# Three gates of a two-stream transformer layer: multiplied on ScalarE, added up on GpSimd, in place of VectorE

## The chip, the cores and the metric

The kernel runs on one core of a Trainium2 chip. The metric is the device time of one execution in microseconds; of before it is the median of three runs. The engines are called PE (TensorE), DVE (VectorE), ACT (ScalarE), POOL (GpSimd) and SP (SyncE, which here only issues transfers).

## The reference

One layer for two streams of 128 tokens by 2048 features, a prompt and a sample. Both go through the same weights, each with its own modulation: a conditioning vector times `w_ada` gives six vectors of 2048 features (a shift, a scale and a gate for the mixer, and the same for the feed-forward part).

```python
def adaln_params(cvec, w_ada_l, b_ada_l):
    mod = jax.nn.silu(cvec) @ w_ada_l + b_ada_l
    return jnp.split(mod[..., None, :], 6, axis=-1)
...
def ffn_residual(x, shift, scale, gate, norm_w, wg, wu, wd):
    h = modulate(rmsnorm(x, norm_w), shift, scale)
    return x + gate * ((jax.nn.silu(h @ wg) * (h @ wu)) @ wd)
...
    sh1, sc1, g1, sh2, sc2, g2 = mods
    hq, hi, hff, hfb, hg, cb, cc, cx, nq, nk, nv = mixer_inputs(x, sh1, sc1, norm_mix_w_l, w_in_l)
...
    x = x + g1 * (jnp.concatenate([o_a, o_b, o_c], axis=-1) @ w_out_l)
    x = ffn_residual(x, sh2, sc2, g2, norm_ffn_w_l, wg, wu, wd)
```

The input projection feeds a gated linear recurrence in both directions, a short convolution and an attention; their outputs go through `w_out`. Everything is float32. The change touches only how parts of `g1` and `g2` are summed.

## The kernel before

The weights (330 MB read in all) stream through once, in tiles of 128 partitions by 2048 values (1 MB), and both streams' products are made from each. A float32 product is made of three float32r ones: SP loads a tile into `raw` (four buffers), ACT copies each half of it to `hi` rounded to float32r (L253, L296), DVE subtracts (`lo = raw - hi`, L254, L297), and PE multiplies with both (L262 in `products`, L311 in `feature_mm`). `hi` and `lo` have three buffers each, of half a tile (1024 values a partition).

In time: first norm, the first modulation and input projection to about 555 us, output projection to 640, second norm, then the channel mixer: gate and up weights of six of the eleven hidden tiles (650 to 919 us), down weights (to 1050), gate and up of the other five (to 1274), down (to 1383), last norm.

The modulation has 24 chunks of 512 features. The first eight (first shift and scale) are made ahead of all. The later ones are made beside the stream: behind each tile of weights `behind` calls `pump` (one step of every generator that waits) and `ada_step`, which takes parts from two queues at a pace that a table sets for each phase. `LATER_T` goes to PE (`later_pe`). `LATER_V`, seven chunks that are gates (8 to 11 of the output projection, 21 to 23 of the down projection), goes to DVE in `later_dve`: each chunk in eight parts. A part loads two rows of 128 of `w_ada` (`araw`, 512 KB, two buffers) by a transfer that POOL issues (L415), behind a copy of two elements (L414) that marks the buffer, and then DVE does four sums (L418), for two rows and two streams:

```python
nc.vector.scalar_tensor_tensor(acc[:, s, :], raw[:, k, :], cs[:, 2 * part + k, s:s + 1], acc[:, s, :],
                               op0=ALU.mult, op1=ALU.add)
```

So each partition sums its own rows into `acc` (`aacc`, one buffer). After the eighth part `later_gate` splits the sum as well (ACT L376, DVE L377), PE adds over the partitions with a matrix of ones (L382), and ACT copies the gate out (L383). In all 56 parts and 224 sums.

Instructions on each engine run in the order that a scheduler gave them at build time; it simulates the program and lets weights' steps go ahead of others by a priority. An engine that waits for an instruction's operands holds everything behind it.

`u4` is a ring of tiles of 1024 values for intermediate results, of nine buffers. Two of the chunk-20 quarters are loaded into four of them at the end of the output projection (L924 to L926, on SP's queue).

Of the kernel before, what the change touches and what calls it, by code (L numbers as in the profile page):

```python
# [28 lines left out]
# Chunks of the later modulation that the tensor engine takes (the shift and the scale of the same features in turn),  # L29
# and those that the vector engine takes (gates).  # L30
# [3 lines left out]
RAW_BUFS, HL_BUFS, U8_BUFS, U4_BUFS, ST_BUFS = 4, 3, 10, 9, 4  # L34
# [3 lines left out]
# Tiles of the later modulation per tile of the other weights: in the input projection's last round of the first  # L38
# chunks, its other chunks, the output projection and the channel mixer.
# [4 lines left out]
def pairs(t, m, slot0=0):  # L44
    """View of a [P, 2, n, 128] tile: even blocks of m from the first slot, odd ones from the second."""
    b = t[:, :, :, :]
    n = b.shape[2] * b.shape[3]
    return bass.AP(tensor=b.tensor, offset=b.offset,
                   ap=[list(b.ap[0]), [2 * m, n // (2 * m)], [n + m, 2], [1, m]])
# [9 lines left out]
def half_blocks(t, slot, par, m):  # L59
    """Blocks of m with parity par in one slot of a [P, 2, n, 128] tile: [P, blocks, m]."""  # L60
    b = t[:, :, :, :]
    n = b.shape[2] * b.shape[3]
    return bass.AP(tensor=b.tensor, offset=b.offset + slot * n + par * m,
                   ap=[list(b.ap[0]), [2 * m, n // (2 * m)], [1, m]])


def sibling(t, slot, par, m, nb):
    """Per-block values [P, 2, nb] of one slot and parity, repeated along m: [P, nb / 2, m]."""
    b = t[:, :, :]
    return bass.AP(tensor=b.tensor, offset=b.offset + slot * nb + par,  # L70
                   ap=[list(b.ap[0]), [2, nb // 2], [0, m]])


def sibling_pairs(t, m, nb):
    """Odd values of the first slot, even ones of the second, repeated along m: [P, nb / 2, 2, m]."""
    b = t[:, :, :]
    return bass.AP(tensor=b.tensor, offset=b.offset + 1,
                   ap=[list(b.ap[0]), [2, nb // 2], [nb - 1, 2], [0, m]])


def bc_last(ap, n):
    """[P, a] or [P, a, b] repeated n times along a new last axis."""
    return bass.AP(tensor=ap.tensor, offset=ap.offset, ap=[list(x) for x in ap.ap] + [[0, n]])


def bc_mid(ap, n):
    """[P, a] repeated n times along a new middle axis: [P, n, a]."""
    return bass.AP(tensor=ap.tensor, offset=ap.offset,
                   ap=[list(ap.ap[0]), [0, n]] + [list(x) for x in ap.ap[1:]])
# [3 lines left out]
def trunk(ctx: ExitStack, tc: tile.TileContext, a: dict):  # L93
# [71 lines left out]
    def other_inputs(after):  # L165
        """The small inputs that nothing needs at first; after: a tile that is written first."""
        lvf = st((P, 5, 32))
        selbf = st((P, 2, P))
        for dst, src in ((nfw, a["nfw"]), (gnw, a["gnw"]), (lvf, a["lvl"]), (cvw, a["cvw"]),
                         (selbf, a["selb"])):  # L170
            v = dst if len(dst.shape) == 2 else dst[:, 0, :]
            nc.gpsimd.tensor_copy(v[:, 0:1], after[:, 0:1])
            nc.gpsimd.dma_start(dst, src)
        yield
        yield
        nc.vector.tensor_copy(lvl, lvf)
        nc.vector.tensor_copy(selb, selbf)
        nc.vector.tensor_scalar(ones, ident, 0.0, 1.0, op0=ALU.mult, op1=ALU.add)
        nc.vector.reciprocal(lbs, lbe)
        nc.vector.tensor_tensor(lbe, lbe, lbs, op=ALU.mult)  # L180
        nc.vector.tensor_tensor(lb, lbe, lbe, op=ALU.subtract)
        nc.vector.tensor_scalar(oml, lb, -1.0, 1.0, op0=ALU.mult, op1=ALU.add)

    def rsqrt(v, n):
        """v ** -0.5 of a positive [P, n]: a first guess from the exponent, then Newton's steps."""
        g = sb([P, 8], "rs_g", 2)[:, :n]
        t = sb([P, 8], "rs_t", 2)[:, :n]
        nc.vector.tensor_scalar(g.bitcast(I32), v.bitcast(I32), 1, None, op0=ALU.logical_shift_right)
        nc.vector.tensor_scalar(g.bitcast(I32), g.bitcast(I32), -1.0, float(0x5F3759DF), op0=ALU.mult, op1=ALU.add)
        for _ in range(3):  # L190
            nc.vector.tensor_tensor(t, g, g, op=ALU.mult)
            nc.vector.scalar_tensor_tensor(t, t, -0.5, v, op0=ALU.mult, op1=ALU.mult)
            nc.vector.scalar_tensor_tensor(g, t, 1.5, g, op0=ALU.add, op1=ALU.mult)
        return g

    def rms1(ssq, width, rest=EPS):
        """1 / sqrt(ssq / width + rest) of a [P, 1], times RMS1: Newton's steps without their factors."""
# [14 lines left out]
    def rms(ssq, n, width):  # L212
        """1 / sqrt(ssq / width + eps)."""
        v = sb([P, 8], "rs_v", 2)[:, :n]
        nc.vector.tensor_scalar(v, ssq, 1.0 / width, EPS, op0=ALU.mult, op1=ALU.add)
        return rsqrt(v, n)

    def most(ssq):
        """All sums of squares but the last, as rms1 adds them."""
        t = sb([P, 1], "most", 2)  # L220
        nc.vector.tensor_reduce(t, ssq, axis=AX.X, op=ALU.add)
        nc.vector.tensor_scalar(t, t, 1.0 / D, EPS, op0=ALU.mult, op1=ALU.add)
        return t

# [13 lines left out]
    def split(src, apart=False):  # L238
        """The two float32r parts of a tile of weights, two rows of 128 at a time."""
# [18 lines left out]
    def products(acc, s, k, lhs, lk, parts, first, last):  # L258
        """acc += lhs[s][lk] @ row k of a tile of weights; lhs: [P, s, hi/lo, 4, 128]."""
        hi, lo = parts[k // 2]  # L260
        for i, (x, w) in enumerate(((0, hi), (1, hi), (0, lo))):
            nc.tensor.matmul(acc, lhsT=lhs[:, s, x, lk, :], rhs=w[:, k % 2, :],  # L262
                             start=first and i == 0, stop=last and i == 2)

    def split_mm(src, acc, lhs, first, last, k0=0):
        """acc[s] += lhs[s][k] @ src[:, k]; src: [P, k, 512] of DRAM; lhs: [P, s, hi/lo, 4, 128], from its k0 on."""
# [6 lines left out]
    def last_mm(steps, acc, phase):  # L273
        """The last of a sum, one stream after the other; yields the stream that is done."""
# [10 lines left out]
    def feature_mm(src, rhs, accs2, first, last):  # L285
        """accs2[b] += src[:, k, b].T @ the tokens; src: [P, 8, 256] of DRAM.

        rhs(k): either [P, 512], their two parts, that stay apart, or two of [P, s, 128], that are summed."""
# [30 lines left out]
    def ada_pe(src, box, part, pieces, first, last):  # L319
        """A quarter of a chunk of the modulation on the tensor engine, in four parts g.  # L320

        pieces: (columns, row): the chunk's columns whose sums go to rows 32 g + row + s."""
# [21 lines left out]
    def columns(e, n):  # L344
        """[P, 128 n]: the sums of two modulations in its rows -> [P, n, 2 and 2] by features."""
# [21 lines left out]
    def later_gate(c, parts, pe):  # L367
        """parts[s]: [P, 512] whose sum over partitions (those of s) is the modulation."""
# [19 lines left out]
    def later_pe(c, part, box):  # L388
        """A quarter of a chunk on the tensor engine: a gate, or the second shift and scale, both into one sum."""
# [14 lines left out]
    def later_dve(c, part, box):  # L404
        """An eighth of a gate's chunk on the vector engine, each partition summing its own rows."""
# [10 lines left out]
        for k in range(2):  # L416
            for s in range(2):
# [31 lines left out]
    def behind(phase=None):  # L449
        """What follows a tile of weights."""  # L450
# [4 lines left out]
    def transposes(src):  # L455
        """[128 tokens, 512] in SBUF -> [128, 4, 128] in PSUM."""
# [6 lines left out]
    def split_fm(dst, s, src):  # L463
        """dst: [P, s, hi/lo, 4, 128] tile; src: [P, 4, 128], in PSUM or SBUF."""
# [3 lines left out]
    def norm_fm(xn, diag=None):  # L468
        """xn[s]: [128, 256] in SBUF -> [128, s, 2, 128] in PSUM, its tokens scaled by a diagonal matrix."""
# [9 lines left out]
    def modulated(dst, ps, layer, v):  # L479
        """The modulated norm's features 256 v .. of both streams into dst."""  # L480
# [30 lines left out]
    hT = [None] * 4  # L511

    def first_mod(v, part, box):
        """The first shift and scale of 256 features, a quarter of the sum at a time, and what they modulate."""
# [31 lines left out]
    def heads(t, h):  # L546
        """Head h of a [P, (s, 4 heads), 128] tile: [P, s, 128]."""
# [421 lines left out]
    def hidden(c, f):  # L969
        """256 features of the hidden layer, by features, into a half of f."""  # L970
# [37 lines left out]
    for gi, grp in enumerate(groups):  # L1008
# [6 lines left out]
        for n in range(4):  # L1015
# [8 lines left out]
            for s in last_mm([(a["w_down"][n, grp[j]], fs[j]) for j in range(many, len(grp))], acc, 3):  # L1024
# [105 lines left out]
```

## Time and profile before

| | us |
|---|---|
| median of three runs | 1398.59 (1397.38 to 1398.76) |
| span of the profiled execution | 1393.3 |
| PE busy | 1352.9 |
| DVE busy | 908.2 |
| ACT busy | 652.5 |
| POOL busy | 138.9 |

The profile gives the profiled execution by its span, from the first instruction to the last; no device time of that one execution stands beside it. The span is 5.3 us under the median of the runs. The page's second part cuts the span into 40 slices of 34.8 us: PE shows 9 (90% or more) in 38 of them, and DVE's digits are 8 or 9 in the slices of the input projection, where its other work meets the gates' sums, and 5 to 6 in the last third.

In the rows below, an instruction is named by its line in the code, the engine, the operation, and what it writes `<-` what it reads.

### The profile page before, as it was taken

The page shows a single profiled execution, that of the slowest core. Times are in us where ns is not written, and L with a number is a line of the kernel's source. Part 1 is how long each engine was busy: PE and PEld are TensorE (multiplying, and loading weights), DVE is VectorE, ACT ScalarE, POOL GpSimd, SP SyncE. Part 2 cuts the span into 40 slices and gives each one's busy share as a digit, 9 for nine tenths or more (in the row PEclk, how much of TensorE's full clock was granted, in tenths as well). Part 3 has the DMA queues.
Part 4 walks back from the last instruction along what each step waited for, and adds up shares of the span by engine and source line. Part 5 has one row for each costly group of instructions (what it writes and reads, how often), then busy time and mean ns, then how long its engine had stood idle before and what let it go on. Part 6 is the DMA issues. An engine that isn't in the chain of part 4 may idle for free. (4 is left out here: it accounts for less than half of the span.)

```text
span 1393.3 us, 21206 instructions
## 1 busy us (share of the span) xinstructions
PE 1352.9 (97%) x8552; PEld 1103.2 (79%) x8552; DVE 908.2 (65%) x1190; ACT 652.5 (47%) x927; POOL 138.9 (10%) x201
## 2 busy tenths in 40 slices
PE   5999999999999999999999999999999999999996
PEld 3666767897897896678888887888888888888885
DVE  3354568987967886468958788555555555555565
ACT  4433347655455433446454444543334444444442
POOL 1000002321222230001202121000000000000000
PEclk9999999999999999999999999999999999999999
DMA  8897877775877898765755666555556555555551
GB/s 349 294 359 273 317 304 272 293 268 212 304 274 264 318 348 317 265 263 198 282 198 213 242 215 230 186 185 189 203 183 220 197 186 181 185 194 196 183 203 67
DMA packets 54386, 335.48 MB, mean 241 GB/s; under 512 B 7248, under 2 KB 7312, under 8 KB 19216
## 3 DMA queue, kind: packets, MB, share of 16 engines
q1 hardware_dynamic: 42768, 296.79, 57.9%
q0 software_dynamic: 10944, 36.29, 7.3%
q8 instruction: 67, 1.10, 0.3%
q10 hardware_dynamic: 576, 1.05, 0.2%
q14 instruction: 31, 0.25, 0.0%
HBM read 330.43 MB, written 3.67 MB: 240 GB/s over the span
## 5 line engine op out<-in xcount | busy, mean ns | idle before, releaser
L311 PE MATMUL acc<-u,hi 128*128 128x512 f32 (+1 forms) x2176 | 629.3, 357 | 0.0
L311 PE MATMUL acc<-u,lo 128*128 128x256 f32 x1792 | 488.4, 282 | 6.1 <-DVE lo L297 6.1
L262 PE MATMUL acc<-hi,u 128*128 128x512 f32 x1536 | 459.0, 394 | 2.1 <-ACT u L491 1.4
L311 PEld LDWEIGHTS acc<-u,hi 128*128 128x128 f32 x2176 | 378.5, 189 | 63.3 <-issue 5.9
L254 DVE TENSOR_TENSOR lo<-raw,hi 128x1024 fp32r<-128x1024 f32 x192 | 234.2, 1223 | 204.6 <-ACT hi L253 204.6
L297 DVE TENSOR_TENSOR lo<-raw,hi 128x1024 fp32r<-128x1024 f32 x224 | 273.7, 1223 | 140.1 <-ACT hi L296 137.1
L311 PEld LDWEIGHTS acc<-u,lo 128*128 128x128 f32 x1792 | 337.4, 189 | 21.4 <-DVE lo L297 10.7
L296 ACT ACTIVATE hi<-raw 128x1024 fp32r<-128x1024 f32 x224 | 237.0, 1059 | 243.3 <-PE acc L311 179.9
L262 PEld LDWEIGHTS acc<-hi,u 128*128 128x128 f32 x1536 | 285.3, 188 | 82.4 <-issue 11.6
L253 ACT ACTIVATE hi<-raw 128x1024 fp32r<-128x1024 f32 x192 | 202.1, 1059 | 289.4 <-PE acc L262 207.8
L262 PE MATMUL acc<-lo,u 128*128 128x512 f32 x768 | 280.5, 394 | 0.5 <-DVE lo L254 0.5
L418 DVE SCALAR_TENSOR_TENSOR aacc<-araw,cs,aacc 128x512 f32<-128x512 f32 x224 | 160.1, 747 | 36.5 <-DMA araw<-w_ada 30.2
L262 PEld LDWEIGHTS acc<-lo,u 128*128 128x128 f32 x768 | 142.1, 188 | 40.5 <-issue 6.6
L335 PE MATMUL ada<-raw,cst 128*32 128x256 f32 (+1 forms) x784 | 91.8, 478 | 11.6 <-DMA raw<-w_ada 11.6
L414 POOL COPY araw<-u 128x2 f32<-128x2 f32 x56 | 58.7, 1049 | 265.0 <-DVE aacc L418 217.1
L987 ACT ACTIVATE st<-acc 128x256 f32<-128x256 f32 x88 | 33.3, 379 | 66.7 <-PE acc L311 66.7
L335 PEld LDWEIGHTS ada<-raw,cst 128*32 128x32 f32 x784 | 26.4, 112 | 44.0 <-issue 30.7
L885 DVE TENSOR_TENSOR u<-u,acc 128x512 f32<-128x512 f32 x56 | 37.6, 684 | 25.0 <-PE acc L262 24.9
L988 DVE TENSOR_TENSOR st<-st,acc 128x256 f32<-128x256 f32 x88 | 36.8, 418 | 20.4 <-ACT st L987 20.4
L415 POOL DMA_DIRECT2D araw<-w_ada x56 | 30.0, 536 | 15.5 <-POOL araw L414 15.5
L408 POOL COPY aacc<-u 128x2 f32<-128x2 f32 x7 | 3.1, 446 | 237.0 <-DVE u L885 171.6
L487 ACT ACTIVATE st<-aux,sh,sc 128x128 f32<-128x128 f32 x48 | 18.0, 457 | 11.8 <-DVE sc L356 7.2
(222 smaller groups left out, 651.2 us busy)
## 6 DMA issues: line engine op xcount, KB each, us to landing
raw<-w_ada SPq DMA_DIRECT2D x66, 1024.0 KB, 7.1
raw<-w_gate SPq DMA_DIRECT2D x44, 1024.0 KB, 4.8
raw<-w_up SPq DMA_DIRECT2D x44, 1024.0 KB, 4.9
raw<-w_down SPq DMA_DIRECT2D x44, 1024.0 KB, 4.8
raw<-w_in SPq DMA_DIRECT2D x33, 1024.0 KB, 6.4
araw<-w_ada POOLq DMA_DIRECT2D x56, 512.0 KB, 5.7
raw<-w_infm SPq DMA_DIRECT2D x24, 1024.0 KB, 6.8
raw<-w_out SPq DMA_DIRECT2D x16, 1024.0 KB, 5.8
```

What stands on the lines that cost most here:

```text
L253: nc.scalar.activation(hi, raw[:, 2 * j:2 * j + 2], AF.Copy)
L254: nc.vector.tensor_tensor(lo, raw[:, 2 * j:2 * j + 2], hi.bitcast(F32), op=ALU.subtract)
L262: nc.tensor.matmul(acc, lhsT=lhs[:, s, x, lk, :], rhs=w[:, k % 2, :], start=first and i == 0, stop=last and i == 2)
L296: nc.scalar.activation(hi, raw[:, 4 * j:4 * j + 4], AF.Copy)
L297: nc.vector.tensor_tensor(lo, raw[:, 4 * j:4 * j + 4], hi.bitcast(F32), op=ALU.subtract)
L311: nc.tensor.matmul(dst, lhsT=w[:, k % 4, ws], rhs=y, start=first and k == 0 and i == 0, stop=last and k == 7 and i == len(todo) - 1)
L335: nc.tensor.matmul(box["acc"][32 * k:32 * k + 32, 0:cols.stop - cols.start], lhsT=cst[:, 4 * part + k, 2 - row:34 - row], rhs=raw[k // 2][ ...
L414: nc.gpsimd.tensor_copy(raw[:, :, 0:1], S["late"][:, :, 0:1])
L418: nc.vector.scalar_tensor_tensor(acc[:, s, :], raw[:, k, :], cs[:, 2 * part + k, s:s + 1], acc[:, s, :], op0=ALU.mult, op1=ALU.add)
L885: nc.vector.tensor_tensor(part[name][:, s, :], part[name][:, s, :], acc[s], op=ALU.add)
L987: nc.scalar.activation(t[:, b], acc[b][:, 256:512], AF.Copy)
L988: nc.vector.tensor_tensor(t[:, b], t[:, b], acc[b][:, 0:256], op=ALU.add)
```

## The change

`LATER_AP` names three of DVE's seven gates: 9, 11 and 22. For these a part's four sums are taken apart: ACT multiplies each row by both streams' conditioning values (L421 into a new tile `at` of two buffers, L422 into `araw` itself), and POOL adds the two products to `acc` (L424). That is 32 multiplications and 32 additions for each of the three gates, 96 of either, in place of 96 sums on DVE. The room for `at` is taken from the ring `u4`, which goes from nine buffers to eight. Nothing else in the program's work changes; lines from L28 on shift by two, and by nine behind the change.

```diff
 LATER_V = [8, 9, 10, 11, 21, 22, 23]
 LATER_GAP = 20
-RAW_BUFS, HL_BUFS, U8_BUFS, U4_BUFS, ST_BUFS = 4, 3, 10, 9, 4
+
+LATER_AP = [9, 11, 22]
+RAW_BUFS, HL_BUFS, U8_BUFS, U4_BUFS, ST_BUFS = 4, 3, 10, 8, 4
...
         for k in range(2):
+            if c in LATER_AP:
+                t = sb([P, CH], "at", 2)
+                nc.scalar.activation(t, raw[:, k, :], AF.Copy, scale=cs[:, 2 * part + k, 0:1])
+                nc.scalar.activation(raw[:, k, :], raw[:, k, :], AF.Copy, scale=cs[:, 2 * part + k, 1:2])
+                for s, v in enumerate((t, raw[:, k, :])):
+                    nc.gpsimd.tensor_tensor(acc[:, s, :], acc[:, s, :], v, op=ALU.add)
+                continue
             for s in range(2):
                 nc.vector.scalar_tensor_tensor(acc[:, s, :], raw[:, k, :], cs[:, 2 * part + k, s:s + 1], acc[:, s, :],
                                                op0=ALU.mult, op1=ALU.add)
```

The scheduler's order moves with it. On ACT, in the channel mixer, where gate 22 is summed, the row before reads as follows: `hi` copies of the gate and up weights (L296), and the hidden layer's own steps (L987 out of PSUM, L996, L991).

```order
L987 ACTIVATE st_7071<-acc_6975 128x256
L296 ACTIVATE hi_7136<-raw_7130 128x1024
L296 ACTIVATE hi_7182<-raw_7180 128x1024
L996 ACTIVATE u_1036_6859<-st_6968 128x2x256
L296 ACTIVATE hi_7186<-raw_7180 128x1024
L987 ACTIVATE st_7172<-acc_7079 128x256
L296 ACTIVATE hi_7231<-raw_7229 128x1024
L987 ACTIVATE st_7172<-acc_7080 128x256
L296 ACTIVATE hi_7235<-raw_7229 128x1024
L991 ACTIVATE st_7172<-st_7172 128x512
```

After, at the same place (L298 is the `hi` copy, L996 and L1000 are the hidden layer's):

```order
L298 ACTIVATE hi_7363<-raw_7361 128x1024
L996 ACTIVATE st_7298<-acc_7200 128x256
L421 ACTIVATE at_7246<-araw_7243,cs 128x512
L421 ACTIVATE at_7251<-araw_7243,cs 128x512
L422 ACTIVATE araw_7243<-araw_7243,cs 128x512
L298 ACTIVATE hi_7367<-raw_7361 128x1024
L422 ACTIVATE araw_7243<-araw_7243,cs 128x512
L1000 ACTIVATE st_7298<-st_7298 128x512
L421 ACTIVATE at_7351<-araw_7348,cs 128x512
L298 ACTIVATE hi_7429<-raw_7427 128x1024
L421 ACTIVATE at_7356<-araw_7348,cs 128x512
L422 ACTIVATE araw_7348<-araw_7348,cs 128x512 x2
```

The multiplications stand in groups of two to four between the `hi` copies, and a `hi` stands directly behind one that writes an `at` tile.

On DVE, the same place before: `lo` (L297), the gate's sums (L418), the hidden layer's steps (L988, L997).

```order
L418 SCALAR_TENSOR_TENSOR aacc_6792<-araw_7222,cs,aacc_6792 128x512
L997 TENSOR_TENSOR u_1036_6859<-st_6968,u_1036_6859 128x2x256
L297 TENSOR_TENSOR lo_7187<-raw_7180,hi_7186 128x1024
L418 SCALAR_TENSOR_TENSOR aacc_6792<-araw_7222,cs,aacc_6792 128x512
L988 TENSOR_TENSOR st_7172<-st_7172,acc_7079 128x256
L418 SCALAR_TENSOR_TENSOR aacc_6792<-araw_7222,cs,aacc_6792 128x512
L297 TENSOR_TENSOR lo_7232<-raw_7229,hi_7231 128x1024
L988 TENSOR_TENSOR st_7172<-st_7172,acc_7080 128x256
L418 SCALAR_TENSOR_TENSOR aacc_6792<-araw_7222,cs,aacc_6792 128x512
L418 SCALAR_TENSOR_TENSOR aacc_6792<-araw_7271,cs,aacc_6792 128x512
L297 TENSOR_TENSOR lo_7236<-raw_7229,hi_7235 128x1024
```

After, L299 is `lo` and L997 the step out of PSUM:

```order
L299 TENSOR_TENSOR lo_7364<-raw_7361,hi_7363 128x1024
L997 TENSOR_TENSOR st_7298<-st_7298,acc_7200 128x256
L299 TENSOR_TENSOR lo_7368<-raw_7361,hi_7367 128x1024
L299 TENSOR_TENSOR lo_7430<-raw_7427,hi_7429 128x1024
L299 TENSOR_TENSOR lo_7434<-raw_7427,hi_7433 128x1024
L997 TENSOR_TENSOR st_7416<-st_7416,acc_7304 128x256
L299 TENSOR_TENSOR lo_7485<-raw_7482,hi_7484 128x1024
L997 TENSOR_TENSOR st_7416<-st_7416,acc_7305 128x256
```

The sums are gone from between the `lo` steps, and nothing took their place.

On POOL, in the input projection, where gate 9 is summed, before: copies that mark a buffer, and transfers of `w_ada`.

```order
L414 COPY araw_3210<-u_411_2649 128x2
L415 DMA araw_3210<-w_ada 128x1024
L414 COPY araw_3382<-u_495_3217 128x2
L415 DMA araw_3382<-w_ada 128x1024
L414 COPY araw_3468<-u_495_3217 128x2
L415 DMA araw_3468<-w_ada 128x1024
L414 COPY araw_3562<-u_495_3217 128x2
L415 DMA araw_3562<-w_ada 128x1024
```

After (L416 and L417 are the copy and the transfer):

```order
L416 COPY araw_3406<-u_503_3241 128x2
L417 DMA araw_3406<-w_ada 128x1024
L424 TENSOR_TENSOR aacc_2943<-aacc_2943,at_3231 128x512
L424 TENSOR_TENSOR aacc_2943<-aacc_2943,araw_3228 128x512
L424 TENSOR_TENSOR aacc_2943<-aacc_2943,at_3236 128x512
L424 TENSOR_TENSOR aacc_2943<-aacc_2943,araw_3228 128x512
L424 TENSOR_TENSOR aacc_2943<-aacc_2943,at_3409 128x512
L416 COPY araw_3498<-u_503_3241 128x2
L424 TENSOR_TENSOR aacc_2943<-aacc_2943,araw_3406 128x512
L424 TENSOR_TENSOR aacc_2943<-aacc_2943,at_3414 128x512
L417 DMA araw_3498<-w_ada 128x1024
L424 TENSOR_TENSOR aacc_2943<-aacc_2943,araw_3406 128x512
```

The copies and transfers now stand between additions, and the transfer for a later part is queued behind additions of an earlier one.

On SP's queue the fourth transfer of the chunk-20 tiles (L926 before) moves behind the mixer's first tile of gate weights; on PE, rows of the input projection shift by half a tile near 230 to 260 us. Both come from the smaller `u4` ring.

## Rows read from the trace of the kernel before

**Rows 1.** The page's part 1: busy time and share of the span.

```profile
PE 1352.9 (97%) x8552; PEld 1103.2 (79%) x8552; DVE 908.2 (65%) x1190; ACT 652.5 (47%) x927; POOL 138.9 (10%) x201
```

**Rows 2.** Groups by form: busy us, mean ns | idle us before <-releasers.

```profile
L418 DVE SCALAR_TENSOR_TENSOR aacc<-araw,cs,aacc 128x512 f32<-128x512 f32 x224 | 160.1, 747 | 36.5 <-DMA araw<-w_ada 30.2 <-DMA aacc<-b_ada 6.2
...
L296 ACT ACTIVATE hi<-raw 128x1024 fp32r<-128x1024 f32 x224 | 237.0, 1059 | 243.3 <-PE acc L311 179.9 <-issue 34.3 <-PE acc L262 18.0
...
L1047 ACT ACTIVATE u<-u,r_g 128x512 f32<-128x512 f32 x4 | 2.7, 714 | 4.1 <-DVE r_g L207 4.1
...
L414 POOL COPY araw<-u 128x2 f32<-128x2 f32 x56 | 58.7, 1049 | 265.0 <-DVE aacc L418 217.1 <-DVE u L885 21.8 <-DVE u L492 14.1
```

**Rows 3.** The chain of waits, in order of time: start us, us, what.

```profile
838.05 2.39 POOL araw L414
...
840.74 6.08 DMA araw<-w_ada
...
848.88 19.47 PE acc L311 x110
...
1049.74 224.09 PE acc L311 x1280
```

**Rows 4.** Windows of the three stretches: length; PE, PEld, DVE, ACT, POOL busy; clock.

```profile
339.60:402.80 63.20, 62.30 (x731) 52.15 (x729) 57.00 (x84) 30.80 (x57) 17.74 (x23) 1.00 0.76 280
477.90:549.30 71.40, 71.40 (x478) 59.62 (x478) 56.35 (x79) 27.26 (x34) 12.61 (x22) 1.00 0.87 330
733.50:798.80 65.30, 62.20 (x342) 52.87 (x341) 52.28 (x69) 29.29 (x39) 13.62 (x16) 0.97 0.67 240
```

**Rows 5.** Timeline of PE, 757 to 778: start us, us, instruction [idle before <-releaser].

```profile
760.73 0.50 PE L311 MATMUL acc<-u,lo 128*128 128x256 f32 x2 [1.16 <-DVE lo L297]
...
764.85 0.40 PE L311 MATMUL acc<-u,hi 128*128 128x512 f32 x1
...
775.14 0.50 PE L311 MATMUL acc<-u,lo 128*128 128x256 f32 x2 [1.93 <-DVE lo L297]
...
776.60 0.63 PE L311 MATMUL acc<-u,hi 128*128 128x512 f32 x1
```

**Rows 6.** Timeline of DVE (first five) and POOL, 744 to 782 us.

```profile
755.87 0.41 DVE L988 TENSOR_TENSOR st<-st,acc 128x256 f32<-128x256 f32 x1
...
758.79 0.75 DVE L418 SCALAR_TENSOR_TENSOR aacc<-araw,cs,aacc 128x512 f32<-128x512 f32 x1 [2.51 <-DMA araw<-w_ada]
...
763.66 1.41 DVE L418 SCALAR_TENSOR_TENSOR aacc<-araw,cs,aacc 128x512 f32<-128x512 f32 x2
...
765.59 1.22 DVE L297 TENSOR_TENSOR lo<-raw,hi 128x1024 fp32r<-128x1024 f32 x1
...
773.19 0.75 DVE L418 SCALAR_TENSOR_TENSOR aacc<-araw,cs,aacc 128x512 f32<-128x512 f32 x1 [2.60 <-DMA araw<-w_ada]
...
756.02 0.19 POOL L414 COPY araw<-u 128x2 f32<-128x2 f32 x1 [2.65 <-DVE aacc L418]
...
764.47 2.38 POOL L414 COPY araw<-u 128x2 f32<-128x2 f32 x1 [7.44 <-DVE aacc L418]
```

**Rows 7.** Windows of the same three stretches, L418 alone: their sum and mean.

```profile
sum 199.90, DVE 67.28; mean DVE 22.43
```

**Rows 8.** Groups by form on POOL.

```profile
L409 POOL MEMSET aacc<- 128x1024 f32 x7 | 6.7, 957 | 0.4
...
masks.py:199 POOL TENSOR_SCALAR_AFFINE_SELECT ident<-ident 128x128 f32<-128x128 f32 x1 | 0.3, 304 | 0.1
...
masks.py:197 POOL MEMSET ident<- 128x128 f32 x1 | 0.2, 205 | 0.0
```

**Rows 9.** Groups by form on DVE, 339.6 to 402.8; the last row, 733.5 to 798.8.

```profile
L635 DVE COPY_PREDICATED st<-lvl,aux 128x256 f32<-128x256 uint8 x4 | 1.8, 442 | 0.0
...
L695 DVE TENSOR_TENSOR st<-aux,u 128x512 f32<-128x512 f32 x2 | 1.4, 686 | 0.0
...
L988 DVE TENSOR_TENSOR st<-st,acc 128x256 f32<-128x256 f32 x10 | 4.2, 415 | 1.1 <-ACT st L987 1.1
```

## The prediction, made before the changed kernel ran

> **What bounds the kernel now.** I read the busy times first. TensorE (PE) is busy 97% of the span, VectorE (DVE) 65%, ScalarE (ACT) 47%, GpSimd (POOL) 10% [rows 1]. So DVE has time over as a mean, and taking 96 x 0.747 = 71.7 us of sums from it [rows 2] shortens nothing by itself. I read the chain of waits next: from 848.88 us on it is PE (its longest piece is 224.09 us without a break), and ahead of that stand a POOL copy of 2.39 us and a transfer of 6.08 us for a gate's sum, that is, the sum (L418) was late and the next `lo` (L297) stood behind it on DVE [rows 3]. So the question is where `lo` or `hi` reaches PE late, as each half tile of weights goes raw -> `hi` (ACT, 1.06 us [rows 2]) -> `lo` (DVE, 1.22 us [rows 6]) -> PE.
>
> The cover: 1280 matmuls in 224.09 us [rows 3] are 80 half tiles, 2.80 us of PE each. There are three buffers of `hi` and `lo`; while PE works on two, the third has 2 x 2.80 - 1.06 - 1.22 = 3.3 us to spare (an estimate: it supposes that PE frees a buffer just as ACT wants it). A step on ACT or DVE may be late by so much before PE stands.
>
> Next come the three stretches in which the changed gates are summed: 339.6 to 402.8 us (gate 9), 477.9 to 549.3 (gate 11), 733.5 to 798.8 (gate 22), found by counting the `hi` copies between which the new order puts their work. PE is busy 62.3 of 63.2 us, 71.4 of 71.4, and 62.2 of 65.3 [rows 4]. Only in gate 22's does PE stand: 1.16 us at 760.73 and 1.93 us at 775.14, both times waiting for `lo` [rows 5]. Just ahead of each, DVE stood 2.51 and 2.60 us in L418 waiting for `araw`'s transfer [rows 6], the `lo` behind it. After the second pause the same matmul takes 0.63 us where it took 0.40 [rows 5], and the granted clock of the stretch is 0.97, a fall of the clock that I put at 1.0 us (an estimate: 0.03 x 65.3 would be 2.0, of which the pauses themselves hold a part). So the change can win 1.16 + 1.93 + 1.0 = 4.1 us here, and nothing elsewhere.
>
> **The change, part by part.** *Removed:* 32 sums of each of the three gates from DVE, 22.4 us a stretch [rows 7]. DVE's remainder is 57.0 - 22.4 = 34.6, 33.9 and 29.9 us [rows 4, 7].
>
> *ACT:* 32 multiplications a gate. The nearest row is ACT's 128x512 copy with a scale per partition, 714 ns [rows 2]: 22.8 us a stretch, on 30.8, 27.3 and 29.3 us [rows 4]. ACT goes to some 54 of 63.2 us. That fits, so its price is zero as long as nothing on it waits. But ACT works in order, and it carries `hi`: a multiplication (L421) that waits for one of the two `at` tiles, or for `araw`'s transfer, has the next `hi` behind it, then `lo`, then PE. Before, a late gate held up `lo`; now it holds up `hi`, one step further from PE.
>
> *POOL:* 32 additions a gate. No row has one, so I bound it. POOL's memsets of 128 and 1024 elements take 205 and 957 ns [rows 8], that is 0.10 us and 0.84 ns an element. One pass over 512 elements would be 0.53 us, three passes (two operands read, one written) 1.39 us. The one POOL row that reads and writes a large tile, the AFFINE_SELECT of 128 elements, takes 304 ns [rows 8], or 1.6 ns an element: 0.92 us for 512, with the second operand still to come. I take the middle of 0.92 and 1.39, 1.15 us, since an addition lies above that row, and keep 0.53 and 1.39 as ends. The Trainium skill (GPSIMD Engine Reference, 3.1 Elementwise) gives 4497 ns for 2048 elements; a quarter is an estimate of 1.12 us, by which the sum below would be 1.0 us lower.
>
> *Taking turns:* POOL's copies of two elements (L414) show what a read on POOL does beside DVE. At 756.02 one takes 0.19 us, while DVE is in an operation with an operand in PSUM (L988). At 764.47 one takes 2.38 us and ends at 766.85, with DVE's train of operations on two SBUF operands (from L418 at 763.66 to the end of L297 at 766.81) [rows 6]. The 56 copies average 1.05 us [rows 2]. So POOL's reads don't overlap those operations, and 32 additions must find their time beside what remains of them: 34.6 less L695's 1.4 and L635's 1.8 us, which have an operand in PSUM, is 31.4 us in the first stretch; 29.9 less L988's 4.2 is 25.7 in the third [rows 9]; for the second I take off the mean of these, 3.7: 30.2. The additions are 32 x 1.15 = 36.8 us, eight copies 8 x 0.19 = 1.5 us.
>
> That rows show a wait only to the end of a train of DVE's operations speaks for POOL losing each contest. The Trainium skill (SBUF — State Buffer, Who interferes with whom) says otherwise: such a DVE operation and a GpSimd instruction that reads SBUF exclude each other, the later one waiting for a single instruction of the other. The copy of 2.38 us outlasted three DVE operations, so that part isn't what the trace shows; whether DVE in turn waits for POOL, no row here can show, the copies being too short. By either the two kinds of work must be added, and the sum below is the same.
>
> *The sum.* Gate 9: 31.4 + 36.8 + 1.5 = 69.7 us of turns in 63.2: 6.5 late, less the cover of 3.3: 3.2 us of PE standing, and behind it the slow clock of 1.0 us, as behind 775 us: **+4.2 us**. Gate 11: 30.2 + 38.3 = 68.5 in 71.4: fits, 0. Gate 22: 25.7 + 38.3 = 64.0 in 65.3 - 4.1 = 61.2: 2.8 late, which the cover takes: 0 new. But its old pauses stay: a part's transfer is issued when the last sum of two parts before is done, and a sum that ends on POOL (1.15 us, turns aside) ends no earlier than one of 0.747 us did. So `araw` lands no sooner, the wait of 2.5 us moves from DVE to ACT, and takes `hi` along. Saved: 0 of 4.1 us. The sum is 1393.3 + 4.2 = 1397.5 us of span. The span before stands 5.3 us under the median of the runs shown, 1398.59; added to that, **1402.8 us**.
>
> *Small edits.* The ring `u4` goes from 9 to 8 buffers: one gap tile's transfer moves behind the first tile of the mixer on SP's queue, where the output projection ends, and PE's order shifts by half a tile where the first features are projected: zero, covered by the raw tiles under way (four buffers); a transfer like `araw`'s that came too late, 6.08 us [rows 3], less the 2.80 us of a half tile, would cost some 3 us. In the first stretch POOL's queue also holds seven copies and issues of attention inputs (L729 to L737), which the additions ahead of them would make later; they move no large tile, so they cost POOL's time but hardly a turn: zero, and some 3 us of POOL's time if it has none to spare.
>
> **The rivals.** *A, the forecast*: POOL sets the pace in gate 9, gate 22's pauses stay. With the addition between 1.05 and 1.25 us, 69.7 becomes 66.5 (the cover takes it, nothing lost) to 72.9 (6.4 us and the clock's 1.0); there gate 22 is 67.2 - 61.2 - 3.3 = 2.7 us over as well: its own range 1399 to 1409. For it: DVE's load in these stretches is at 80 to 90%, and the copies show that POOL has to wait for it. Against it: additions may wait only to begin and then run beside DVE. Chance 0.42.
>
> *B, faster*: the addition is near one pass (0.53 to 0.8 us), or overlaps DVE once begun. At 0.8 gate 9 needs 31.4 + 25.6 + 1.5 = 58.5 of 63.2, everything fits, POOL keeps ahead of ACT, ACT never waits for `at`, and `lo` has DVE to itself: gate 22's pauses go. 1398.6 - 4.1 = 1394.5 us. This is the one on the other side; it decides at an addition of (63.2 - 31.4 - 1.5) / 32 = 0.95 us. For it: PE has no other losses there and DVE sheds 40% of its work. Against: at AFFINE_SELECT's rate one operand alone would already take 0.92. Chance 0.25.
>
> *C, no change*: POOL fits in gate 9 or runs late within the cover, but the transfer's wait merely moves to ACT: neither +4.2 nor -4.1, or half of each. 1398.6 us, 1396 to 1401. For it: `araw` still has two buffers, and a transfer of 6.08 us [rows 3] is what L418 waited for. Chance 0.20.
>
> *D, much slower*: three full passes, 1.39 us. Turns are 77.4, 76.2 and 71.7 us in 63.2, 71.4 and 61.2: 10.9 + 1.5 + 7.2 us over the cover, less the 4.1, is +15.5: 1414.1 us. Chance 0.13.
>
> **How the numbers follow.** A measurement of this kernel can tell about 0.2%, 2.8 us, from no change: the bounds are 1395.8 and 1401.4. B lies below; C and A's lowest part between (0.20 + 0.05); the rest of A and D above. Faster 0.25, same 0.25, slower 0.50. Since both signs have weight, the range takes in B's 1394.5 and D's 1414.1: 1394 to 1415; left out is little more than POOL being worse than three passes. A's own range is 1399 to 1409.
>
> **What would show it.** In the changed kernel's profile: additions (L424) of 1.15 us when DVE is idle, 1.5 to 2 with waiting, POOL near 90% busy in 340 to 403 us; DVE at 55% there; ACT's idle time ahead of L421 released by POOL L424; PE idle ahead of L299/L311 released by `hi` or `lo`, 3 us more than before by 410 us, with a lower clock behind it, and nothing more at 480 to 550. At gate 22 ACT's L421 waits for `araw<-w_ada`. The forecast is wrong if additions take under 0.9 us, if DVE's `lo` and the additions overlap in the records, if PE's pauses at 760 and 775 are gone, or if the loss lies where no gate of 9, 11 and 22 is summed.

## The result: slower, by more than the range allowed

The changed kernel takes 1435.18 us (median, 1433.73 to 1437.67) beside 1397.99 us for the kernel before on the same chip: a ratio of 1.0277, with a 95% interval of 1.0256 to 1.0298, some 37 us. The direction of the prediction was right, its size (1402.8, at most 1415) was not.

The page of the changed kernel, part 1 and the slices of part 2 (one digit for 36 us of the span, busy share in tenths; PEclk is the granted clock):

```profile
PE 1362.1 (95%) x8552; PEld 1107.9 (77%) x8552; DVE 909.9 (63%) x1094; ACT 708.8 (49%) x1023; POOL 280.0 (20%) x297
...
PE   4999999999789998999999899999999999999997
...
DVE  3354568978766667667966778655555555556555
...
POOL 0100001116672257410115952000000000000000
PEclk9999999999899999999999999999999999999999
```

Beside [rows 1], DVE has lost 96 sums of 71.7 us and is busy 1.7 us *longer*. Apart from the first and the last slice, PE's digits fall below 9 only where POOL's rise: at gates 9 and 11, and at gate 22. The windows between the same `hi` copies that bounded [rows 4] (columns as there) are 86.2, 77.4 and 69.6 us long instead of 63.2, 71.4 and 65.3:

```profile
344.10:430.30 86.20, 70.75 (x752) 56.62 (x752) 65.09 (x58) 51.42 (x98) 65.07 (x56) 0.90 0.57 209
508.40:585.80 77.40, 70.39 (x453) 58.17 (x452) 53.39 (x48) 44.95 (x64) 57.70 (x57) 0.98 0.76 289
770.00:839.60 69.60, 61.75 (x341) 51.17 (x340) 46.97 (x36) 45.18 (x66) 60.71 (x46) 1.00 0.56 197
```

In gate 9's, 23.0 us longer than before, PE stands 86.2 - 70.75 = 15.5 us and is busy 8.5 us longer than in [rows 4], with 752 matmuls in the window for 731: the mean granted clock fell to 0.90. In gate 11's PE stands 7.0 us, where it stood 0. In gate 22's the clock is back at 1.00, but PE stands 7.9 us against 3.1. The three windows hold 33.3 of the 42.6 us by which the span grew (1393.3 to 1435.9). The other 9.3 us lie outside them: by the windows' bounds 4.5 us ahead of gate 9's, 3.0 us between it and gate 11's, 1.8 us behind gate 22's. DVE's remainder, 34.6 us in the forecast, has become 65.1 us in the first window.

Why DVE is busy longer is plain in two timelines of the changed kernel, POOL's additions and DVE at the start of gate 9 (start us, us, instruction):

```profile
342.95 2.28 POOL L424 TENSOR_TENSOR aacc<-aacc,araw 128x512 f32<-128x512 f32 x1
345.19 2.29 POOL L424 TENSOR_TENSOR aacc<-aacc,at 128x512 f32<-128x512 f32 x1
347.44 2.27 POOL L424 TENSOR_TENSOR aacc<-aacc,araw 128x512 f32<-128x512 f32 x1
...
395.53 1.26 POOL L424 TENSOR_TENSOR aacc<-aacc,at 128x512 f32<-128x512 f32 x1 [5.99 <-ACT at L421]
```

```profile
341.75 2.32 DVE L256 TENSOR_TENSOR lo<-raw,hi 128x1024 fp32r<-128x1024 f32 x1
343.99 2.32 DVE L672 TENSOR_TENSOR u<-u,st 128x1024 f32<-128x1024 f32 x1
346.24 2.32 DVE L256 TENSOR_TENSOR lo<-raw,hi 128x1024 fp32r<-128x1024 f32 x1
348.48 0.45 DVE L644 COPY_PREDICATED st<-lvl,aux 128x256 f32<-128x256 uint8 x1
```

An addition alone takes 1.26 us (395.53, with DVE idle), a `lo` alone 1.22 us. Side by side each takes about 2.3 us: its own time, and the rest of one instruction of the other engine ahead of it. The COPY_PREDICATED, which has an operand in PSUM, keeps its 0.45 us. So in these rows the two take turns, one instruction each, and waiting counts as busy in both engines' rows.

The other new wait is ACT's. Two rows of ACT, and PE's three longest idle times in the first two windows:

```profile
363.22 1.33 ACT L421 ACTIVATE at<-araw,cs 128x512 f32<-128x512 f32 x2 [11.99 <-DMA araw<-w_ada]
...
394.72 1.33 ACT L421 ACTIVATE at<-araw,cs 128x512 f32<-128x512 f32 x2 [11.22 <-DMA araw<-w_ada]
```

```profile
366.50 0.80 PE L264 MATMUL acc<-hi,u 128*128 128x512 f32 x1 [5.99 <-ACT hi L255]
...
398.75 1.54 PE L468 MATMUL aux<-ident,u 128*128 128x128 f32 x6 [6.57 <-ACT u L919]
...
546.13 0.58 PE L313 MATMUL acc<-u,lo 128*128 128x256 f32 x1 [5.17 <-DVE lo L299]
```

POOL issues a transfer only behind additions; ACT arrives at the multiplication long before the data and holds `hi` (L255) and other copies (L919) behind it for 11 to 12 us. These two pauses behind ACT are 12.6 of the 15.5 us that PE stands in gate 9's window. In gate 11's all 7.0 us, and in gate 22's 6.2 of 7.9, are put down to `lo` on DVE.

### The profile page after: what moved, and what is told of

Read it like the earlier page. It is cut to its first block, busy times and chain, and to the rows that moved or that the text cites. A ratio compares the mean times of both kernels' runs of the same rounds, so it can differ in the third digit from the quotient of the medians.

```text
span 1435.9 us, 21320 instructions
## 1 busy us (share of the span) xinstructions
PE 1362.1 (95%) x8552; PEld 1107.9 (77%) x8552; DVE 909.9 (63%) x1094; ACT 708.8 (49%) x1023; POOL 280.0 (20%) x297
## 5 line engine op out<-in xcount | busy, mean ns | idle before, releaser
L299 DVE TENSOR_TENSOR lo<-raw,hi 128x1024 fp32r<-128x1024 f32 x224 | 302.6, 1355 | 176.9 <-ACT hi L298 175.7
L256 DVE TENSOR_TENSOR lo<-raw,hi 128x1024 fp32r<-128x1024 f32 x192 | 247.3, 1294 | 203.3 <-ACT hi L255 203.0
L255 ACT ACTIVATE hi<-raw 128x1024 fp32r<-128x1024 f32 x192 | 202.1, 1059 | 271.9 <-PE acc L264 172.4
L298 ACT ACTIVATE hi<-raw 128x1024 fp32r<-128x1024 f32 x224 | 236.3, 1057 | 196.9 <-PE acc L313 142.3
L427 DVE SCALAR_TENSOR_TENSOR aacc<-araw,cs,aacc 128x512 f32<-128x512 f32 x128 | 91.2, 744 | 37.0 <-DMA araw<-w_ada 27.9
L416 POOL COPY araw<-u 128x2 f32<-128x2 f32 x56 | 52.2, 935 | 169.8 <-DVE aacc L427 125.6
L424 POOL TENSOR_TENSOR aacc<-aacc,at 128x512 f32<-128x512 f32 x48 | 74.1, 1544 | 36.4 <-ACT at L421 29.1
L424 POOL TENSOR_TENSOR aacc<-aacc,araw 128x512 f32<-128x512 f32 x48 | 77.7, 1618 | 7.6 <-ACT araw L422 7.3
L996 ACT ACTIVATE st<-acc 128x256 f32<-128x256 f32 x88 | 33.3, 378 | 55.6 <-PE acc L313 55.5
L421 ACT ACTIVATE at<-araw,cs 128x512 f32<-128x512 f32 x48 | 32.6, 715 | 56.6 <-DMA araw<-w_ada 50.6
```

The costliest lines, as they stand in the source:

```text
L255: nc.scalar.activation(hi, raw[:, 2 * j:2 * j + 2], AF.Copy)
L256: nc.vector.tensor_tensor(lo, raw[:, 2 * j:2 * j + 2], hi.bitcast(F32), op=ALU.subtract)
L298: nc.scalar.activation(hi, raw[:, 4 * j:4 * j + 4], AF.Copy)
L299: nc.vector.tensor_tensor(lo, raw[:, 4 * j:4 * j + 4], hi.bitcast(F32), op=ALU.subtract)
L416: nc.gpsimd.tensor_copy(raw[:, :, 0:1], S["late"][:, :, 0:1])
L424: nc.gpsimd.tensor_tensor(acc[:, s, :], acc[:, s, :], v, op=ALU.add)
```

## The experiments

Two theories stood against each other, and a third beside them. **T1**: additions delay the release of `araw` and the next transfer, ACT waits for it, `hi` stands behind. **T2**: the additions and DVE's operations take turns, and the time that DVE is held reaches PE. **T3**: the smaller ring and the new order of the schedule cost it. Ratios are to the kernel before on the same chip.

**The ring alone** (`e1_ring8`): all gates on DVE, eight `u4` buffers.

```diff
-LATER_AP = [9, 11, 22]
+LATER_AP = []
```

> All seven gates on DVE again, only the u4 ring stays at eight buffers. Theory T1 (a part's transfer is queued on POOL behind additions, and ACT waits for it with hi behind) and T2 (additions and DVE's lo take turns): nothing of either is left, 1398 us, within 3. Theory T3 (the smaller ring and the new order cost it): most of the 37 us stay, 1420 or more.

1401.96 us, ratio 1.0042 (1.0029 to 1.0056). T3 is a part, 6 us, and no more; the forecast of the change had it at zero. The longest new pause of PE in this run is at 268 us, just behind the stretch whose order had shifted (another, of 1.89 us, is at 405 us):

```profile
268.50 0.50 PE L313 MATMUL acc<-u,lo 128*128 128x256 f32 x2 [2.96 <-DVE lo L299]
```

**Additions of two columns** (`e2_tiny`):

```diff
-                    nc.gpsimd.tensor_tensor(acc[:, s, :], acc[:, s, :], v, op=ALU.add)
+                    nc.gpsimd.tensor_tensor(acc[:, s, 0:2], acc[:, s, 0:2], v[:, 0:2], op=ALU.add)
```

> POOL's 96 additions cover two of 512 columns, so the three gates are wrong; every dependency and ACT's 96 multiplications stay, only the length of an addition (1.26 us alone) goes. T1 and T2 both: 1394 to 1402 us, since the transfers are issued early and DVE isn't held. If ACT's own load or its place ahead of hi were the cause: 1420 or more.

This kernel leaves out all but two of the 512 columns of the three gates' sums. 1409.82 us, ratio 1.0101 (1.0070 to 1.0133): neither expectation. The length of an addition is worth 25 us, but 8 us above the ring's cost stay with the short ones.

**Memsets in place of additions** (`e3_memset`):

```diff
-                    nc.gpsimd.tensor_tensor(acc[:, s, :], acc[:, s, :], v, op=ALU.add)
+                    nc.gpsimd.memset(v, 0.0)
+                    nc.gpsimd.memset(acc[:, s, :], 0.0)
```

> Each addition is replaced by two memsets of 512 columns on POOL (some 1.06 us together by the memset rows), which write the product's tile and the sum, and read nothing; the three gates are zero. POOL's time and order and all waits stay, its reads go. T1: most of the loss stays, 1412 to 1430 us, with ACT waiting for araw. T2: lo at 1.22 us throughout and 1394 to 1402 us.

1404.63 us, ratio 1.0052 (1.0032 to 1.0071), 1 us above the ring, which the intervals can't tell from none. ACT still multiplies ahead of `hi` here, and waits 39.4 us for transfers. I don't take the run as proof against T1: the memset of the product's tile doesn't depend on the sum, so a tile was released after 0.53 us, and for some parts before the sum's buffer was free. `e5` and `e9` mend that.

**Additions on DVE, multiplications on ACT** (`e4_adds_dve`):

```diff
-                    nc.gpsimd.tensor_tensor(acc[:, s, :], acc[:, s, :], v, op=ALU.add)
+                    nc.vector.tensor_tensor(acc[:, s, :], acc[:, s, :], v, op=ALU.add)
```

> ACT multiplies as in the change, DVE adds (a tensor_tensor of 128x512 takes 0.69 us, so DVE is as loaded as before the change). T1: POOL only issues transfers, early; ACT still waits for some of them with hi behind: 1396 to 1406 us. T2: nothing on POOL to take turns with: 1398 us. If ACT's waits for the transfers alone were enough for the loss: 1420 or more.

1411.88 us, ratio 1.0106 (1.0082 to 1.0131), 9 us above the ring and between the expectations. POOL does nothing new here, so this is what the multiplications on ACT cost: ACT waits 46.4 us for transfers with `hi` behind it, and DVE's additions wait 23.9 us in front of `lo`, nearly all for products. The two weren't taken apart. Its ACT timeline and the pause of PE behind it:

```profile
364.29 0.72 ACT L421 ACTIVATE at<-araw,cs 128x512 f32<-128x512 f32 x1 [9.71 <-DMA araw<-w_ada]
```

```profile
367.37 2.08 PE L264 MATMUL acc<-hi,u 128*128 128x512 f32 x4 [4.58 <-ACT hi L255]
```

**POOL as busy and as late, without reading** (`e5_tiny_memset`, and with a third memset `e9_tiny_memset3`): the short addition keeps the dependency on the sum, the memsets behind it hold the tile. The same columns are left out as with the short additions alone.

```diff
-                    nc.gpsimd.tensor_tensor(acc[:, s, :], acc[:, s, :], v, op=ALU.add)
+                    nc.gpsimd.tensor_tensor(acc[:, s, 0:2], acc[:, s, 0:2], v[:, 0:2], op=ALU.add)
+                    nc.gpsimd.memset(v, 0.0)
+                    nc.gpsimd.memset(v, 0.0)
```

> Each addition covers two columns and is followed on POOL by two memsets of 512 columns of the product's tile (0.53 us each): POOL is as busy as with the additions and releases the tiles as late, but reads SBUF only for a moment (the three gates are wrong). T1 (what costs is that POOL's time stands ahead of the release of araw and so of the next transfer, for which ACT waits with hi behind): 1422 to 1440 us, as the change. T2 (what costs is the turns between additions and DVE's operations): 1403 to 1415 us, as with additions of two columns alone, and lo stays at 1.22 us.

> As with two memsets behind each addition of two columns, but three: POOL needs some 0.4 + 1.58 = 2.0 us for a product, more than the 1.58 us of the additions in the change, and reads SBUF as little as before (the three gates are wrong). T1 (POOL's time ahead of the next transfer): 1440 us or more. T2 (turns): POOL's 32 x 2.0 + 12 = 76 us a gate still delay the transfers somewhat, but lo stays at 1.22 us: 1406 to 1422 us.

`e5`: 1407.85 us, ratio 1.0082 (1.0058 to 1.0106). `e9`: 1407.55 us, ratio 1.0103 (1.0075 to 1.0130). Both as with short additions alone. The groups of `e9` (busy us, mean ns | idle before, releaser), and the same ACT and DVE groups of the change behind them:

```profile
L421 ACT ACTIVATE at<-araw,cs 128x512 f32<-128x512 f32 x48 | 33.0, 716 | 61.0 <-DMA araw<-w_ada 50.7 <-POOL at L427 5.1 <-POOL araw L427 3.7
...
L427 POOL MEMSET at<- 128x512 f32 x48 | 25.3, 526 | 0.1
...
L299 DVE TENSOR_TENSOR lo<-raw,hi 128x1024 fp32r<-128x1024 f32 x224 | 273.4, 1223 | 204.6 <-ACT hi L298 202.8 <-PE ada L337 1.7
```

```profile
L421 ACT ACTIVATE at<-araw,cs 128x512 f32<-128x512 f32 x48 | 32.6, 715 | 56.6 <-DMA araw<-w_ada 50.6 <-POOL aacc L424 5.8
...
L424 POOL TENSOR_TENSOR aacc<-aacc,at 128x512 f32<-128x512 f32 x48 | 74.1, 1544 | 36.4 <-ACT at L421 29.1 <-DMA aacc<-b_ada 7.0
...
L299 DVE TENSOR_TENSOR lo<-raw,hi 128x1024 fp32r<-128x1024 f32 x224 | 302.6, 1355 | 176.9 <-ACT hi L298 175.7 <-PE acc L313 1.1
```

In `e9` ACT waits as long for transfers as in the change (50.7 and 50.6 us), and POOL needs 0.34 to 0.45 + 3 x 0.53 = 1.9 to 2.0 us for a product where the change needs 1.54 to 1.62. But `lo` stays at 1223 ns, and 24 us of the loss are gone. Gate 9's stretch in `e9` (columns as [rows 4]) is 72.4 us long, where the change has 86.2 and the kernel before 63.2:

```profile
341.80:414.20 72.40, 67.64 (x757) 56.58 (x756) 42.40 (x60) 50.66 (x96) 57.84 (x133) 0.95 0.64 238
```

So a POOL that is busy and late, but hardly reads, isn't enough: T1 alone falls as the main cause. Its path doesn't. ACT's waits add up to the same, but the longest is 7.4 us in `e9` and 12.0 us in the change, and the change's two longest are the ones behind which PE stood 12.6 us. Additions that turns stretch to 2.3 us also put the next transfer off, so part of T2's cost may reach PE over ACT; no run separates that.

**Multiplications on DVE, additions on POOL** (`e6_mult_dve`):

```diff
-                nc.scalar.activation(t, raw[:, k, :], AF.Copy, scale=cs[:, 2 * part + k, 0:1])
-                nc.scalar.activation(raw[:, k, :], raw[:, k, :], AF.Copy, scale=cs[:, 2 * part + k, 1:2])
+                nc.vector.tensor_scalar(t, raw[:, k, :], cs[:, 2 * part + k, 0:1], None, op0=ALU.mult)
+                nc.vector.tensor_scalar(raw[:, k, :], raw[:, k, :], cs[:, 2 * part + k, 1:2], None, op0=ALU.mult)
```

> The products are made on DVE (a tensor_scalar of one SBUF operand, 0.49 us), POOL adds as in the change: ACT has nothing of the gates but the ends, so hi waits for no transfer; lo stands behind the multiplication's wait as it did before the change. T1 (hi behind ACT's waits for transfers): 1400 to 1412 us. T2 (turns of additions and DVE): 1415 to 1440 us, with lo up to 2.3 us long.

1453.92 us, ratio 1.0402 (1.0361 to 1.0444), above T2's range and far from T1's: with ACT out of it, it is worse. The multiplications, expected at 0.49 us, take part in the turns too:

```profile
L422 DVE TENSOR_SCALAR araw<-araw,cs 128x512 f32<-128x512 f32 x48 | 46.8, 998 | 0.2
...
L421 DVE TENSOR_SCALAR at<-araw,cs 128x512 f32<-128x512 f32 x48 | 35.1, 759 | 31.1 <-DMA araw<-w_ada 27.8 <-POOL aacc L424 3.1
```

**Additions that nobody waits for** (`e12_idle_adds`): the sums on DVE as before, and beside them on POOL

```diff
+        if c in LATER_AP:
+            t = sb([P, CH], "at", 2)
+            nc.gpsimd.tensor_copy(t[:, 0:2], raw[:, 0, 0:2])
+            u = cst.rearrange("p a b -> p (a b)")[:, 0:CH]
+            for _ in range(2):
+                nc.gpsimd.tensor_tensor(t, u, u, op=ALU.add)
         for k in range(2):
```

> All gates summed on DVE as before the change, ring at eight buffers; beside them POOL makes two additions of 128x512 of constants for each part of gates 9, 11 and 22 (48 in all, half the change's number), whose result nobody reads, each pair behind the landing of the part's transfer. If only POOL's own lateness costs: as the run with the smaller ring alone, 1402 us, ratio 1.004, within 0.003. If additions that read SBUF hold DVE's operations (T2): lo up to 2.3 us beside them, and by turns 53.8 + 20.2 + 1.5 = 75.5 us in 63.2 for gate 9 and 69.8 in 61.2 for gate 22, less the cover 9 and 5 us more: 1410 to 1422 us, ratio 1.012 to 1.02.

1415.37 us, ratio 1.0133 (1.0113 to 1.0153), as T2 has it. 48 additions whose result nobody reads cost 13 us above the ring. POOL waits for the part's data ahead of them, and later transfers stand behind it in its queue, but DVE's sums wait for their transfers no longer than with the ring alone, 36.6 and 36.8 us in all (`e1`, then `e12`):

```profile
L427 DVE SCALAR_TENSOR_TENSOR aacc<-araw,cs,aacc 128x512 f32<-128x512 f32 x224 | 160.8, 749 | 41.4 <-DMA araw<-w_ada 36.8 <-DMA aacc<-b_ada 4.5
...
L426 DVE SCALAR_TENSOR_TENSOR aacc<-araw,cs,aacc 128x512 f32<-128x512 f32 x224 | 176.5, 817 | 43.8 <-DMA araw<-w_ada 36.6 <-DMA aacc<-b_ada 6.0 <-POOL at L420 1.1
```

DVE and POOL at one of the additions, and PE behind:

```profile
771.75 2.06 DVE L299 TENSOR_TENSOR lo<-raw,hi 128x1024 fp32r<-128x1024 f32 x1
```

```profile
771.28 1.45 POOL L423 TENSOR_TENSOR at<-cst 128x512 f32<-128x512 f32 x1
```

```profile
773.87 0.79 PE L313 MATMUL acc<-u,lo 128*128 128x256 f32 x2 [3.87 <-DVE lo L299]
```

The `lo` that begins within the addition takes 2.06 us, and PE stood 3.87 us for it (a wait of the sum ahead of it for its transfer, 3.53 us, is the other part). Without POOL's operation reading anything that DVE writes, this shows the hold by itself.

**Doses.** Gate 9 alone (`LATER_AP = [9]`), gate 22 alone (`[22]`), and half of each gate (`e10_half`: the sample's sums stay on DVE):

```diff
-                nc.scalar.activation(raw[:, k, :], raw[:, k, :], AF.Copy, scale=cs[:, 2 * part + k, 1:2])
-                for s, v in enumerate((t, raw[:, k, :])):
-                    nc.gpsimd.tensor_tensor(acc[:, s, :], acc[:, s, :], v, op=ALU.add)
+                nc.gpsimd.tensor_tensor(acc[:, 0, :], acc[:, 0, :], t, op=ALU.add)
+                nc.vector.scalar_tensor_tensor(acc[:, 1, :], raw[:, k, :], cs[:, 2 * part + k, 1:2], acc[:, 1, :],
+                                               op0=ALU.mult, op1=ALU.add)
```

> Gate 9 alone on ACT and POOL, the ring at eight buffers. If the three gates cost as the profile of the change has them (24 us of its 42 between the hi copies of gate 9): 1412 to 1424 us. If gate 9 is late only because of what comes before or if lateness hands on from gate to gate: under 1408 us.

> Gate 22 alone on ACT and POOL, ring at eight buffers. By the prediction's step for it (2.8 us late under a cover of 3.3, old pauses stay) nothing on top of the ring: 1400 to 1403 us. By the shifts in the profile of the change (some 5 us between the hi copies of gate 22) 1404 to 1409 us.

> Half the dose: of the three gates only the prompt's sums go over ACT and POOL (48 multiplications, 48 additions), the sample's stay on DVE. T2: turns in the first stretch are 31.4 + 11.2 + 16 x 1.26 + 1.5 = 64 us in 63, nearly a fit: a third of the full loss or less, 1403 to 1412 us. If the loss goes with the number of additions: half of 37 us, some 1416; if ACT's waits at the head of hi make it, whatever the number: 1410 or more as in the runs without additions on POOL.

Gate 9 alone: 1424.77 us, 1.0197 (1.0153 to 1.0240), 0.8 us above the range that was expected. Gate 22 alone: 1405.97 us, 1.0078 (1.0060 to 1.0096), 5 us above the ring, not 0. Half: 1419.96 us, 1.0190 (1.0165 to 1.0215): half the additions keep more than half of the loss, so the expectation's turns, which nearly fitted, were too kind. Above the short additions' 1.0103 (`e9`) it is 12 us, half of the change's 24, though with half the multiplications as well. DVE's sums of the sample's stream are held as well:

```profile
L423 DVE SCALAR_TENSOR_TENSOR aacc<-araw,cs,aacc 128x512 f32<-128x512 f32 x48 | 62.3, 1297 | 11.6 <-DMA araw<-w_ada 10.4 <-DMA aacc<-b_ada 0.7
```

They are 1297 ns where [rows 2] has 747.

**A third buffer in place of the change** (`e8_dve_araw3`): the sums stay on DVE, and the room taken from `u4` goes to `araw`.

```diff
-LATER_AP = [9, 11, 22]
+LATER_AP = []
...
-        raw = sb([P, 2, CH], "araw", 2)
+        raw = sb([P, 2, CH], "araw", 3)
```

> All gates on DVE, the ring at eight buffers, and the room goes to a third buffer of araw. If the transfers' wait is what PE's pauses at 760, 775, 833 and 847 us come from (6.8 us with what follows them), these go: 5 to 8 us under the run with the smaller ring alone, 1394 to 1397 us. If the transfers are late for another reason (POOL's queue, memory): as that run, 1400 to 1404 us.

1389.90 us, ratio 0.9946 (0.9925 to 0.9967): faster than the kernel before by 0.5%, the fastest here, and 4 us under what was expected. DVE's sums wait 14.0 us for transfers where [rows 2] has 30.2 and `e1`, with the same ring, 36.8, and PE stands nowhere in gate 22's stretch, 59.6 us long instead of 65.3 (columns as [rows 4]):

```profile
L427 DVE SCALAR_TENSOR_TENSOR aacc<-araw,cs,aacc 128x512 f32<-128x512 f32 x224 | 161.1, 748 | 19.8 <-DMA araw<-w_ada 14.0 <-DMA aacc<-b_ada 5.8
```

```profile
742.10:801.70 59.60, 59.60 (x341) 51.98 (x341) 52.44 (x69) 29.15 (x40) 12.56 (x16) 1.00 0.72 263
```

So the pauses of [rows 5] did come from the transfers' wait of [rows 6], and the cure was a buffer, not another engine.

## Why the prediction was right and wrong

**Right: the taking of turns.** From POOL's copies [rows 6] the forecast read that POOL's reads and DVE's operations on two SBUF operands exclude each other. `lo` at 1223 ns under memsets (`e9`) and at up to 2.3 us beside additions (the change) shows it from DVE's side, and `e12` that it costs by itself. Of the two readings that were left open, DVE waits for POOL too, and for one instruction at a time. That is what the Trainium skill (SBUF — State Buffer, Who interferes with whom) says: whichever issues first gets the shared ports for its whole instruction, and the other blocks. The additions' timeline above agrees, 1.26 + 1.0 us. Why the copy in [rows 6] outlasted three operations stays open. The right sign is no proof of it: with short additions the kernel was slower by 1.0% already (`e2`, `e9`), from two terms that the forecast held at zero, the ring and ACT. Without the turns the sign would have been right by luck.

**Roughly right: the addition's own time,** 1.15 us forecast, 1.26 us measured; for gate 9 that is 32 x 0.11 = 3.5 us more. The estimate of 1.12 us, a quarter of the figure in the Trainium skill (GPSIMD Engine Reference, 3.1 Elementwise), was 0.14 us low.

**Wrong: the sum of turns less one cover.** The step "69.7 us of turns in 63.2, less the cover of 3.3" treats a stretch as a tub in which any engine may use any moment. With 1.26 us it gives 73.2 us; the stretch took 86.2, 23.0 us more than before where the forecast had 4.2. POOL was busy 65.07 us of it, 75%, where the forecast looked for near 90%. POOL can't use every moment: a part's transfer leaves behind the additions, and then POOL stands for the data, 5.99 us ahead of 395.53 and 4.11 us ahead of 364.03 alone. Nor can DVE: `hi` comes late behind ACT's waits of 12.0 and 11.2 us, each well over the cover of 3.3. For gate 11 the step said "fits, 0"; its stretch grew by 6.0 us. For gate 22 it said 0; alone it costs 5 us.

**Wrong: the clock as 1.0 us.** In gate 9's window the mean granted clock fell to 0.90. Read in slices of half a microsecond, it is 0.50, the lower of its two levels (1.2 GHz, not 2.4), from 364.6 to 375.2 us and from 395.6 to 402.5 us; each time it fell while PE stood in one of its two longest pauses there, 6.0 and 6.6 us. PE was busy 11.5 us of that, which at 1.00 would have taken half: 5.7 us (an estimate), a quarter of the stretch's loss. At 775 us before, PE was busy 3.4 us at 0.50, 1.7 us by the same reckoning and not 1.0.

**Wrong: ACT's price of zero.** The forecast named the wait with `hi` behind it, but used it only to keep gate 22's old pauses. `e2`, `e4`, `e5` and `e9` put the multiplications on ACT at 6 to 9 us above the ring, whether POOL was late or not (1.0082 to 1.0106 against 1.0042). `e3` has the same multiplications at 1 us (1.0052), so the price isn't fixed; that it goes with each kernel's order and with when the transfers leave is argued, not shown.

**Wrong: the ring as 0**: 6 us. That the shifted order makes it is likely from the pause at 268 us, but no run shows which part of it does. The forecast's "some 3 us" if the cover failed was nearer; `e8`, with the same ring, more than wins it back.

Together, as far as such differences add up: the ring 6 us, the multiplications on ACT some 6 to 9 (1 in `e3`), and the rest, some 24 (the change's 1.0277 against 1.0103 of `e9`; 31 against `e3`), what the additions' reads do beside DVE. Rival B failed because additions do hold DVE; rival D had the size nearer, though for a price that wasn't met (1.39 us). How this rest divides between DVE's own delay and the later transfers for which ACT waits wasn't taken apart; the scheduler gave each of these kernels an order of its own.

## What to carry to other kernels

Before moving elementwise work from VectorE to GpSimd, count which of VectorE's remaining operations have two SBUF operands (in `e6` even multiplications of one were held): they and GpSimd's reads run one after the other, so what was taken off comes back as waiting, here as 2.3 us for a 1.22 us step on the way to PE. A busy share that isn't the bound isn't a reason to move work; ask what its waits are for. Here it was a transfer into one of two buffers, and a third buffer gave 0.5%. In an in-order queue, don't put an instruction that waits for a slow transfer ahead of one that feeds the bottleneck.

## What the runs showed of the hardware

A VectorE multiplication of one SBUF operand by a value per partition (tensor_scalar, 128x512 float32) was held by GpSimd's additions as well: 0.76 to 1.0 us as a mean in `e6` against 0.49 us for L1045's in the kernel before. GpSimd's memsets, which read nothing, kept 526 ns and left `lo` at 1223 ns, so here a GpSimd that only writes left VectorE's subtractions alone; one that reads SBUF held them.
